# Layer 0's mixer: low weight parts by adding transfers, GpSimd's elementwise work on VectorE, table products merged

## The chip, the cores and the metric

The kernel runs on one core of one Trainium2 chip. The metric is the device time of one execution in microseconds (us). PE is TensorE, DVE is VectorE, ACT is ScalarE, POOL is GpSimd, and SP is the queue from which most loads are issued.

## What is computed

A stack of two layers on 256 context and 256 latent tokens of width 1024, all in float32. A layer normalises and modulates its input, makes one wide input projection, feeds four mixers from it, gates and sums their projections, and ends with an MLP. In layer 0 both halves of the tokens go through everything; in layer 1 the context feeds only the states of the first mixer.

```python
for l in range(2):
    h = modulate(rms_norm(x), mod[l])          # shift and scale from c @ w_mod
    z = h @ w_in[l]                            # 5 x 256 mixer inputs, 4 x 1024 gates
    y = [s5(z[0:256]), fnet(z[256:512]), pool(z[512:768]), conv(z[768:1280])]
    x = x + ga1 * (sum(sigmoid(gate[b]) * (y[b] @ w_branch[l][b]) for b in range(4)) @ w_out[l])
    x = x + ga2 * (relu(modulate(rms_norm(x)) @ w1[l]) ** 2 @ w2[l])
```

The S5 mixer is a complex linear recurrence over time with 16 groups of 64 states. The kernel does it in blocks of eight steps: it first makes tables from the parameters (powers of the decay times the input matrix B, and the output matrix C times powers), then multiplies tokens by them, scans over the blocks, and reads out.

## The kernel before, in words

**Split weights.** A weight tile is 128x1024 in float32 (512 KB). It is used as a sum of two parts in fp32r, a rounded high part `hi` and the rest `lo = w - hi`. `mm3` then issues three matmuls for each product: hi by x-high, hi by x-low, lo by x-high. A tile of 512 columns is 24 matmuls of 512 columns, one of a projection (`proj`) six.

**The stream of weights.** Class `Stream` walks one list (`plan`) of all weight tiles in the order of use. `load` (L680) starts the transfer of a tile into one of three raw buffers from SP. `high` (L689) takes a free pair of buffers and lets ACT write `hi` from the raw tile. `low` (L700), some 2.5 us later in the program's own clock, lets DVE write `lo` by a subtraction and gives the raw buffer back. There are four pairs, and a fifth is lent until shortly before the first projection. `take` (L720) hands a finished pair to PE, `release` gives it back.

**The order of work.** The program is written out by hand, engine by engine, with each queue in order. The main line is `layer` (L1285): the order string of L948 names gates (`g`), projections (`q`) and the points where a mixer's result is needed (`y`). Beside it run background tasks (generators) that `pump` (L903) advances between the matmuls of a tile. `pump` keeps an estimate of when each engine will have worked off what was issued; a task goes on only while its engines have less than `lead` microseconds of issued work left, counted from PE's present. `yield "w", t` says that the task goes on t us later.

**The tasks of layer 0's mixer.** `S5.prep` (L116) computes the small parameters on DVE. Then `tables_c` (L311) runs on POOL and `tables_b` (L265) on DVE, side by side: eight halves each, six products of 128x256 per half, followed by transposes or matmuls on PE (`products`), ACT copies and stores to scratch in DRAM (`scr_b`, `scr_c`, `scr_k`). When both are done, `S5L.run` starts: scan tables on POOL, block inputs on PE (`states`), the scan (L550) whose forward direction runs on POOL and whose backward direction runs on DVE, and the readout (L600), which loads `scr_c` again from POOL's queue. Pooling, convolution and the Fourier mixer are further tasks on DVE, PE and ACT. After the Fourier mixer's result is taken, `mods` (L1038) computes the remaining modulation columns on DVE from 80 loads of 512 KB (`w_modt`); it goes on far into the MLP.

**Layer 1's tables** are made by the same `tables_b` and `tables_c` during layer 0's MLP, all on POOL and with single buffers.

## Time and profile before

| what | value |
| --- | --- |
| time, median of 3 runs | 1207.88 us (1205.53 to 1212.44) |
| profiled execution: its own time, its span | 1209.18 us, 1207.2 us |
| PE busy | 1160.9 us (96% of the span) |
| DVE busy | 976.1 us (81%) |
| ACT busy | 517.1 us (43%) |
| POOL busy | 282.9 us (23%) |
| moved by DMA | 211.49 MB, 175 GB/s on average |
| mean granted TensorE clock | 0.986 |

The profiled execution is 1.3 us above the median and has 2.0 us outside its span. Times of rows are counted from the span's start. PE's busy time says where PE had work, not that it was at its peak; the granted clock beside it is a share of 2.4 GHz, so a mean of 0.66 over a stretch is a mixture of 1.2 and 2.4 GHz.

### The profile page before, as it was taken

The numbers are of one execution on the slowest core, as the hardware profiler recorded it, in microseconds if no ns is written. First come the engines' busy times: TensorE is split into PE (matmuls) and PEld (weight loads), VectorE is DVE, ScalarE is ACT, GpSimd is POOL, SyncE is SP. The second block draws the span as 40 slices with busy tenths as digits, with TensorE's granted clock in tenths as the row PEclk, the third lists the DMA queues.
The fourth block names the chain that finished last, engine by engine and source line by source line (L and its number), as shares of the span: only waits on it lengthen the run. The fifth ranks groups of instructions, "written<-read, shape, count | busy, mean of one in ns | idle before, by whom it ended". The sixth has DMA issues, their size and how long they took to land.

```text
span 1207.2 us, 20297 instructions
## 1 busy us (share of the span) xinstructions
PE 1160.9 (96%) x7770; PEld 1009.4 (84%) x7770; DVE 976.1 (81%) x1878; ACT 517.1 (43%) x872; POOL 282.9 (23%) x319
## 2 busy tenths in 40 slices
PE   7999897999999999999999899999899999999997
PEld 5777675777888988888887778898899999999997
DVE  6789989977999769999988883546998788867764
ACT  4534242344324365422332333346544556645543
POOL 0038656000000100166555561020520001000000
PEclk9999999999999999999999999999899999999999
DMA  9543531644674514466578774425554545555551
GB/s 366 225 144 109 180 92 52 229 156 138 212 229 156 173 37 148 140 188 230 186 245 296 249 247 180 130 98 177 173 166 167 159 160 205 177 190 179 189 182 48
DMA packets 66513, 211.49 MB, mean 175 GB/s; under 512 B 7984, under 2 KB 13616, under 8 KB 66416
## 3 DMA queue, kind: packets, MB, share of 16 engines
q1 hardware_dynamic: 55456, 183.84, 45.4%
q10 hardware_dynamic: 7696, 14.56, 3.3%
q0 software_dynamic: 3264, 11.80, 2.9%
q8 instruction: 61, 1.00, 0.3%
q14 instruction: 36, 0.29, 0.1%
HBM read 199.19 MB, written 10.98 MB: 174 GB/s over the span
## 4 chain that ended last, share of the span: by engine, by line
PE 72%; DVE 15%; POOL 3%; DMA 3%; issue 3%; ACT 3%; ACTq 0%; POOLq 0%; DVEq 0%; SPq 0%
PE bank L64 72%; DVE scan L64 5%; DVE parts L64 4%; DVE mixer L64 2%; DVE whole L64 2%; ACT parts L64 2%; POOL tables L64 1%; POOL whole L64 1%; ACT whole L64 1%; DVE windows L64 1%; POOL scan L64 1%; DMA whole<-in_w_in_dram 1%; DMA whole<-in_x_dram 0%; DMA scan<-scr_z 0%; DMA scr_c<-tables 0%
## 5 line engine op out<-in xcount | busy, mean ns | idle before, releaser
L64 PE MATMUL bank<-parts 128*128 128x512 f32 (+2 forms) x4008 | 727.2, 339 | 19.0 <-DVE parts L64 16.6
L64 PEld LDWEIGHTS bank<-parts 128*128 128x128 f32 x4008 | 616.3, 191 | 105.4 <-DVE parts L64 22.3
L64 ACT ACTIVATE parts<-whole 128x1024 fp32r<-128x1024 f32 (+1 forms) x288 | 273.7, 959 | 144.9 <-PE bank L64 73.9
L64 DVE TENSOR_TENSOR parts<-whole,parts 128x1024 fp32r<-128x1024 f32 (+1 forms) x240 | 294.0, 1233 | 16.0 <-ACT parts L64 15.6
L64 PE MATMUL bank<-hidden,parts 128*128 128x256 f32 (+1 forms) x1440 | 251.2, 335 | 0.0
L64 PEld LDWEIGHTS bank<-hidden,parts 128*128 128x128 f32 x1440 | 217.5, 188 | 29.9 <-issue 0.3
L64 DVE SCALAR_TENSOR_TENSOR whole<-whole 128x1024 f32<-128x1024 f32 (+4 forms) x188 | 175.7, 936 | 15.2 <-DMA whole<-in_w_modt_dram 12.0
L64 POOL TENSOR_TENSOR whole<-whole 128x256 f32<-128x256 f32 (+1 forms) x69 | 50.3, 743 | 347.2 <-ACT whole L64 342.2
L64 DVE SCALAR_TENSOR_TENSOR whole<-bank,whole 128x256 f32<-128x256 f32 (+1 forms) x121 | 54.7, 475 | 66.4 <-PE bank L64 66.2
L64 ACT ACTIVATE whole<-whole 128x256 f32<-128x256 f32 (+2 forms) x139 | 48.9, 388 | 107.2 <-DVE whole L64 96.4
L64 ACT ACTIVATE mixer<-bank 128x512 f32<-128x512 f32 (+1 forms) x84 | 40.7, 496 | 119.8 <-PE bank L64 110.3
L64 DVE TENSOR_TENSOR whole<-whole 128x256 f32<-128x256 f32 (+7 forms) x158 | 73.0, 467 | 16.7 <-ACT whole L64 11.7
L64 ACT ACTIVATE whole<-bank 128x512 f32<-128x512 f32 (+2 forms) x69 | 35.5, 537 | 109.1 <-PE bank L64 77.5
L64 POOL TENSOR_TENSOR tables<-tables,whole 128x256 f32<-128x256 f32 x48 | 61.4, 1287 | 37.4 <-DMA scr_c<-tables 34.9
L64 DVE TENSOR_TENSOR hidden<-whole,hidden 128x512 fp32r<-128x512 f32 (+2 forms) x77 | 53.4, 698 | 9.0 <-ACT hidden L64 2.4
L64 ACT ACTIVATE hidden<-whole 128x512 fp32r<-128x512 f32 (+2 forms) x77 | 47.1, 615 | 8.2 <-PE bank L64 2.3
L64 ACT ACTIVATE tables<-bank 128x512 f32<-128x512 f32 (+2 forms) x20 | 8.4, 422 | 92.8 <-PE bank L64 92.5
L64 POOL COPY whole<-whole 128x32 f32<-128x32 f32 x20 | 11.9, 626 | 150.3 <-DVE whole L64 150.3
L64 POOL TENSOR_TENSOR scan<-scan,whole 128x256 f32<-128x256 f32 (+3 forms) x50 | 44.0, 892 | 12.0 <-DVE scan L64 8.3
L64 DVE SCALAR_TENSOR_TENSOR scan<-scan,whole 128x512 f32<-128x512 f32 (+1 forms) x64 | 42.7, 728 | 0.0
L64 PE MATMUL bank<-merged,parts 128*128 128x256 f32 (+1 forms) x240 | 38.0, 316 | 0.8 <-DVE merged L64 0.8
L64 DVE TENSOR_TENSOR scan<-scan,whole 128x256 f32<-128x256 f32 (+5 forms) x61 | 31.5, 543 | 9.0 <-ACT whole L64 8.0
(115 smaller groups left out, 899.0 us busy)
## 6 DMA issues: line engine op xcount, KB each, us to landing
whole<-in_w_dram SPq DMA_DIRECT2D x128, 512.0 KB, 4.3
whole<-in_w_in_dram SPq DMA_DIRECT2D x84, 512.0 KB, 4.3
whole<-in_w_modt_dram SPq DMA_DIRECT2D x78, 512.0 KB, 4.1
whole<-in_w_br_dram SPq DMA_DIRECT2D x16, 512.0 KB, 4.4
whole<-in_w_out_dram SPq DMA_DIRECT2D x16, 512.0 KB, 4.2
mixer<-in_w_mod_dram SPq DMA_DIRECT2D x8, 512.0 KB, 9.7
scan<-scr_b POOLq DMA_DIRECT2D x8, 512.0 KB, 5.2
scan<-in_w_mod_dram SPq DMA_DIRECT2D x6, 512.0 KB, 9.7
```

The source lines that it names most:

```text
L64: return f(out, *a, **k)
```

## The change

In layer 0, from the ninth weight tile on up to the fourth output tile, `lo` is no longer made by DVE. ACT writes `hi`, then `-hi` into the low buffer, and a transfer from POOL's queue adds the weight tile from DRAM to what lies there. The raw buffer is free as soon as `-hi` has been issued.

`tables_b` and `tables_c` form their products for real and imaginary part at once: ACT first lays out the four operands (five or six small copies for each half), then three products of 128x512 follow in place of six of 128x256. This holds for both layers; layer 0's `tables_c` moves from POOL to DVE, and so do its scan tables and the forward direction of its scan. The sign change of C goes to ACT.

The tasks' waits change: after a table's products the task goes on when DVE is estimated to be done (`"at"`, `"u"`), the lead of DVE is 6.0 us and of ACT 3.2 us up to the S5 result of layer 0, and the readout gives its loads 12.5 us in place of 10.0.

```diff
+    def turned(self, E, out, x, y, P, space):
+        sh, t = [128, 4, 16, 8], self.K.tmp()
+        w = []
+        for i, p in enumerate(P):
+            w.append(space[:, 32 * i:32 * i + 32])
+            self.K.nc.scalar.activation(w[i].rearrange("p (r q s) -> p r q s", r=2, q=2),
+                                        bc(p[:, None], [128, 2, 2, 8]), AF.Copy)
...
+        E.tensor_tensor(ov, bc(x[:, :, :, None], sh), wv[0], op=MUL)
+        E.tensor_tensor(tv, bc(y[:, :, :, None], sh), wv[1], op=MUL)
+        E.tensor_tensor(out, out, t, op=ADD)
@@ tables_b
-            E.tensor_tensor(ba[:, 0], Bb[0], Pb[0], op=MUL)
-            E.tensor_tensor(tmp, Bb[1], Pb[1], op=MUL)
-            E.tensor_tensor(ba[:, 0], ba[:, 0], tmp, op=SUB)
-            E.tensor_tensor(ba[:, 1], Bb[0], Pb[1], op=MUL)
-            E.tensor_tensor(tmp, Bb[1], Pb[0], op=MUL)
-            E.tensor_tensor(ba[:, 1], ba[:, 1], tmp, op=ADD)
+            nc.scalar.activation(x, bb[:, :, k, qs], AF.Copy)
+            nc.scalar.activation(y[:, 0], bb[:, 1, k, qs], AF.Copy, scale=-1.0)
+            nc.scalar.activation(y[:, 1], bb[:, 0, k, qs], AF.Copy)
+            self.turned(E, BAs[i % nb], space[:, 0:64].rearrange("p (a c) -> p a c", a=4),
+                        space[:, 64:128].rearrange("p (a c) -> p a c", a=4), P, space[:, 128:192])
...
+                yield "at", done[i + 1 - nb] + 0.5
@@ tables_c
-            E.tensor_scalar(CC[:, 1], CC[:, 1], -1.0, 0.0, op0=MUL, op1=ADD)
+            nc.scalar.activation(CC[:, 1], CC[:, 1], AF.Copy, scale=-1.0)
@@ Stream
+        self.added = (8, self.index(("out", 0, 4)))
...
-                self.K.nc.scalar.activation(self.used[i][0][0], self.raw[i], AF.Copy)
+                hi, lo = self.used[i][0]
+                self.K.nc.scalar.activation(hi, self.raw[i], AF.Copy)
                 self.nhigh += 1
-                self.due.append(self.K.nc.clock["t"] + self.lag)
+                if self.adds(i):
+                    self.K.nc.scalar.activation(lo, hi, AF.Copy, scale=-1.0)
+                    self.free.append(self.raw.pop(i))
+                    self.due.append(self.K.nc.clock["t"])
+                    self.low()
+                else:
+                    self.due.append(self.K.nc.clock["t"] + self.lag)
...
-            raw = self.raw.pop(i)
-            self.K.nc.vector.tensor_sub(lo, raw, hi)
-            self.free.append(raw)
+            if self.adds(i):
+                self.K.nc.gpsimd.dma_start(lo, self.plan[i][1], accum_op=ADD)
+            else:
+                raw = self.raw.pop(i)
+                self.K.nc.vector.tensor_sub(lo, raw, hi)
+                self.free.append(raw)
@@ Model, layer, run
-        self.lead = dict(d=2.0, a=2.0, p=5.0)
+        self.lead = dict(d=6.0, a=3.2, p=5.0)
...
+                    self.lead = dict(d=2.0, a=2.0, p=5.0)
...
-            self.tab0.append(self.start(self.pre[0].tables_c(half[1], nc.gpsimd), "pa", 2.5))
+            self.tab0.append(self.start(self.pre[0].tables_c(half[1], nc.vector), "da", 2.5))
@@ readout, S5L
-                yield "w", 10.0
+                yield "w", 12.5
...
-        s.E = [K.nc.gpsimd, K.nc.vector]
+        s.E = [K.nc.gpsimd if l else K.nc.vector, K.nc.vector]
...
-            yield from s.scan_tables(nc.gpsimd)
+            yield from s.scan_tables(nc.vector)
```

How the order moves on POOL, at the place where layer 0's tables stood. In the names, `parts` holds the pairs of high and low parts, `scan` the tables and the states of layer 0's S5, `whole` the constants, raw tiles and temporaries. Before:

```order
L64 COPY whole<-whole 128x32 x9
L64 MEMSET scan 128x256 x2
L64 TENSOR_SCALAR scan<-scan 128x64
L64 TENSOR_TENSOR scan<-scan,whole 128x256
L64 TENSOR_TENSOR whole<-scan,whole 128x256
L64 TENSOR_TENSOR scan<-scan,whole 128x256 x2
```

With the change:

```order
L64 DMA parts<-in_w_in_dram 128x1024 x3
L64 COPY whole<-whole 128x32 x9
L64 DMA parts<-in_w_in_dram 128x1024
L64 DMA parts<-in_w_br_dram 128x1024
L64 DMA parts<-in_w_in_dram 128x1024 x6
L64 DMA parts<-in_w_br_dram 128x1024
L64 DMA parts<-in_w_in_dram 128x1024
L64 DMA scan<-scr_b 128x2x512 x2
L64 DMA scan<-scr_z 128x16x64
```

The products have left POOL. Its queue is now a chain of adding transfers, with the scratch loads of S5 among them, and nine copies of table powers stand ahead of all but the first three. In all 46 weight tiles get an adding transfer.

On DVE, in the middle of the same tables, where one projection's two merges fall. Before:

```order
L64 TENSOR_TENSOR scan<-scan,whole 128x256
L64 TENSOR_TENSOR mixer<-bank_65,mixer 128x512
L64 TENSOR_TENSOR parts<-whole,parts 128x1024
L64 TENSOR_TENSOR mixer<-bank_66,mixer 128x512
L64 TENSOR_TENSOR parts<-whole,parts 128x1024
L64 TENSOR_TENSOR scan<-whole 128x256
L64 TENSOR_TENSOR whole<-whole 128x256
L64 TENSOR_TENSOR scan<-scan,whole 128x256
```

With the change:

```order
L64 TENSOR_TENSOR scan<-scan,whole 128x512
L64 SCALAR_TENSOR_TENSOR scan<-scan,whole 128x512
L64 TENSOR_TENSOR mixer<-bank_65,mixer 128x512
L64 SCALAR_TENSOR_TENSOR scan<-scan,whole 128x512
L64 TENSOR_TENSOR mixer<-bank_66,mixer 128x512
L64 TENSOR_TENSOR scan<-scan 128x512
L64 TENSOR_TENSOR whole<-scan 128x512
L64 TENSOR_TENSOR scan<-scan,whole 128x512
```

The subtractions of 128x1024 (`parts<-whole,parts`) are gone from between the merges, the table products are twice as wide, and convolution steps (`SCALAR_TENSOR_TENSOR`) now stand among them.

## Rows read from the trace of the kernel before

**Rows 1.** Busy time by stage; columns are named in its first line.

```profile
core 0: us, PE busy (x) PEld busy (x) DVE busy (x) ACT busy (x) POOL busy (x), PEclk, DMA share, GB/s
75.00:212.00 137.00, 121.32 (x718) 94.57 (x717) 127.54 (x220) 49.40 (x123) 92.87 (x112) 0.95 0.32 109
212.00:400.00 188.00, 188.00 (x1090) 149.77 (x1089) 166.90 (x264) 69.00 (x96) 2.62 (x5) 0.99 0.57 190
640.00:700.00 60.00, 55.79 (x285) 43.99 (x285) 51.85 (x71) 20.71 (x36) 38.29 (x33) 0.97 0.79 264
```

**Rows 2.** Waits of PE's matmuls, stretch 70 to 215 us: total, times, longest.

```profile
PE bank L64 <- DVE parts L64: 7.8, 1, 7.8
PE bank L64 <- POOL scan L64: 3.9, 2, 2.1
PE bank L64 <- DMA scan<-scr_z: 2.2, 1, 2.2
PE bank L64 <- DVE scan L64: 1.6, 2, 1.0
```

**Rows 3.** Busy time by stretches of 5 us, columns as in rows 1.

```profile
70.00:75.00 5.00, 5.00 (x24) 4.13 (x23) 3.84 (x16) 2.06 (x3) 1.61 (x3) 1.00 0.61 196
...
130.00:135.00 5.00, 5.00 (x18) 3.87 (x16) 4.93 (x8) 3.39 (x6) 3.78 (x5) 0.66 0.27 105
...
210.00:215.00 5.00, 3.58 (x9) 2.82 (x10) 4.96 (x8) 0.15 (x1) 1.86 (x3) 0.50 0.41 135
```

**Rows 4.** Groups of DVE instructions, 75 to 212 us: busy us, mean ns.

```profile
L64 DVE TENSOR_TENSOR parts<-whole,parts 128x1024 fp32r<-128x1024 f32 x14 | 17.8, 1280 | 4.8 <-ACT parts L64 4.8
L64 DVE TENSOR_TENSOR scan<-scan,whole 128x256 f32<-128x256 f32 x22 | 15.9, 722 | 0.6
L64 DVE TENSOR_TENSOR scan<-whole 128x256 f32<-128x256 f32 x16 | 12.5, 782 | 0.0
L64 DVE TENSOR_TENSOR whole<-whole 128x256 f32<-128x256 f32 x16 | 12.3, 769 | 0.6 <-POOL scan L64 0.6
```

**Rows 5.** DVE in order of time: start us, us, instruction.

```profile
77.41 0.69 DVE L64 TENSOR_TENSOR scan<-scan,whole 128x512 f32<-128x512 f32 x1 [3.51 <-ACT whole L64]
...
115.43 0.95 DVE L64 TENSOR_TENSOR scan<-whole 128x256 f32<-128x256 f32 x1
...
121.34 0.41 DVE L64 TENSOR_TENSOR scan<-whole 128x256 f32<-128x256 f32 x1
...
175.18 1.81 DVE L64 TENSOR_TENSOR scan<-scan 128x512 f32<-128x512 f32 x1
...
210.06 0.69 DVE L64 TENSOR_TENSOR scan<-scan 128x512 f32<-128x512 f32 x1
```

**Rows 6.** Groups of ACT instructions, 75 to 212 us.

```profile
L64 ACT ACTIVATE parts<-whole 128x1024 fp32r<-128x1024 f32 x16 | 16.9, 1058 | 5.2 <-DMA whole<-in_w_in_dram 5.1
L64 ACT ACTIVATE mixer<-bank 128x512 f32<-128x512 f32 x19 | 11.4, 598 | 24.0 <-PE bank L64 23.1 <-ACT scan L64 0.8
...
L64 ACT ACTIVATE whole<-whole 128x16 f32<-128x16 f32 x25 | 2.7, 200 | 10.2 <-POOL whole L64 10.2
```

**Rows 7.** The page's DMA queues and issues: count, KB each, us to landing.

```profile
q1 hardware_dynamic: 55456, 183.84, 45.4%
...
mixer<-in_w_mod_dram SPq DMA_DIRECT2D x8, 512.0 KB, 9.7
scan<-scr_b POOLq DMA_DIRECT2D x8, 512.0 KB, 5.2
```

**Rows 8.** Groups of POOL instructions, 75 to 212 us.

```profile
L64 POOL COPY whole<-whole 128x32 f32<-128x32 f32 x7 | 5.7, 848 | 6.6 <-DVE whole L64 6.6
...
L64 POOL DMA_DIRECT2D scan<-scr_b x4 | 3.1, 766 | 17.8 <-PE bank L64 12.7 <-DMA scr_k<-scan 5.1
```

**Rows 9.** Groups of POOL instructions in layer 1's tables, 500 to 720 us.

```profile
L64 POOL TENSOR_TENSOR tables<-tables,whole 128x256 f32<-128x256 f32 x45 | 58.4, 1305 | 37.3 <-DMA scr_c<-tables 34.9
```

**Rows 10.** Waits of matmuls, stretch 630 to 700 us.

```profile
PE bank L64 <- POOL tables L64: 4.2, 3, 3.0
```

More of the change, by code (lines that the diff above doesn't have):

```diff
@@ L262, in powers @@
             yield
+    def turned(self, E, out, x, y, P, space):
[5 more added lines that the diff above has]
+                                        bc(p[:, None], [128, 2, 2, 8]), AF.Copy)
+        ov, tv = [o.rearrange("p (a c s) -> p a c s", a=4, c=16) for o in (out, t)]
+        wv = [bc(v.rearrange("p (a s) -> p a s", a=4)[:, :, None, :], sh) for v in w]
+        E.tensor_tensor(ov, bc(x[:, :, :, None], sh), wv[0], op=MUL)
+        E.tensor_tensor(tv, bc(y[:, :, :, None], sh), wv[1], op=MUL)
+        E.tensor_tensor(out, out, t, op=ADD)
     def tables_b(self, A, E):
@@ L273, in tables_b @@
         nb = 2 if l == 0 else 1
-        BAs, BATs = [A(512) for _ in range(nb)], [A(512) for _ in range(nb)]
+        BAs, BATs, spaces = [[A(w) for _ in range(nb)] for w in (512, 512, 192)]
         def products(i):
@@ L300, in tables_b @@
                 yield "w", 8.0
+            done.append(nc.clock["d"])
             if i >= nb - 1:
+                yield "at", done[i + 1 - nb] + 0.5
                 products(i + 1 - nb)
@@ L319, in tables_c @@
         nb = 2 if l == 0 else 1
-        CCs, CAs, KKs, BLs = [[A(w) for _ in range(n)] for w, n in ((128, 2), (512, nb), (240, nb), (256, nb))]
+        CCs, CAs, KKs, BLs, spaces = [[A(w) for _ in range(n)]
+                                     for w, n in ((128, nb), (512, nb), (240, nb), (256, nb), (192, nb))]
         for BL in BLs:
@@ L324, in load @@
         def load(u):
-            (nc.gpsimd if l else nc.sync).dma_start(CCs[u % 2], K.I["s5c"][l][u])
-        load(0)
-        load(1)
+            (nc.gpsimd if l else nc.sync).dma_start(CCs[u % nb], K.I["s5c"][l][u])
+        for u in range(nb):
+            load(u)
         yield "w", 2.6
@@ L354, in products @@
             nc.scalar.dma_start(K.KD[l][64 * u:64 * u + 64], KK[0:64])
-            if u < 2:
-                load(u + 2)
+            if u + nb < 4:
+                load(u + nb)
         def bufs(u, k):
-            CC = CCs[u % 2].rearrange("p (r k q c) -> p r k q c", r=2, k=2, c=16)
+            CC = CCs[u % nb].rearrange("p (r k q c) -> p r k q c", r=2, k=2, c=16)
             BL = BLs[u % nb].rearrange("p (k r q x) -> p k r q x", k=2, r=2, x=32)
@@ L376, in tables_c @@
                 P = [(base[:, r, 0, qs, 1:9] if k == 0 else rev[:, r, 1, qs, 0:8]) for r in range(2)]
[L377 to L385 removed]
+                space = spaces[(2 * u + k) % nb]
+                x, y = [space[:, j:j + 64].rearrange("p (r q c) -> p r q c", r=2, q=2) for j in (0, 64)]
+                nc.scalar.activation(x, CC[:, :, k], AF.Copy)
+                nc.scalar.activation(y[:, 0], CC[:, 1, k], AF.Copy)
+                nc.scalar.activation(y[:, 1], CC[:, 0, k], AF.Copy, scale=-1.0)
+                self.turned(E, CA, space[:, 0:64].rearrange("p (a c) -> p a c", a=4),
+                            space[:, 64:128].rearrange("p (a c) -> p a c", a=4), P, space[:, 128:192])
                 yield
@@ L388, in tables_c @@
                     yield "w", 8.0
-                todo.append((u, k))
+                todo.append((u, k, nc.clock["d"]))
                 if len(todo) == nb:
-                    products(*todo.pop(0))
+                    if nb > 1:
+                        yield "at", todo[0][2] + 0.5
+                    products(*todo.pop(0)[0:2])
                 if nb == 1:
-                    yield "w", 2.0
-        yield "w", 3.0
+                    yield "w", 2.0 + 2.0 * k
         for x in todo:
-            products(*x)
+            yield "at", x[2] + 0.5
+            products(*x[0:2])
         yield "w", 3.79
@@ L678, in lend, with adds @@
         self.lent.insert(0, (until, slots))
+    def adds(self, i):
+        return self.added[0] <= i < self.added[1]
     def load(self):
@@ L925, in said @@
                 task["cls"] = y[1]
+            elif y[0] == "u":
+                c = self.nc.clock
+                task["ready"] = max(c["t"], c[y[1]]) + y[2]
+            elif y[0] == "at":
+                task["ready"] = y[1]
             else:
@@ L1437, in layer @@
         self.flush()
-        tconv = self.start(br.conv(), "d", 4.0)
+        tconv = self.start(br.conv(), "d", 4.0 if l else 4.0)
         tasks = {2: task, 3: tconv}
@@ L1692, in run @@
         self.pre = [S5(self, 0), None]
-        half = [self.A5.sub(3600), self.A5.sub(2400)]
+        half = [self.A5.sub(3552), self.A5.sub(2656)]
         self.tab0 = []
@@ L1826, in pool @@
             yield
-        yield "w", 3.0
+        yield "u", "d", 0.5
         out = self.bufs_pool()
```

28 lines of the change are left out of this document (10 added, 18 removed).

## The prediction

> **What bounds the kernel now.** I read the table of stages first, then what PE waited for, then the groups of each engine. PE is busy in all but 46 us of the span, so only its idle time and its slow clock can be won. From 212 to 400 us, where most of layer 0's gates and projections run, PE is busy in all 188 us; nothing is to be won there. From 75 to 212 us, while S5's tables, states and scan are made, PE is busy in 121.3 of 137 us and DVE in 127.5 [rows 1]: 15.7 us of PE are lost while DVE is 93% busy. PE's waits name the same engines: 7.8 us once for a low part (`DVE parts`), 3.9 for POOL's tables, 2.2 for the load of S5's input, 1.6 for DVE's tables [rows 2]. Each stall costs twice. In 130 to 135 us, after one of the waits for POOL, the granted clock is 0.66, and in 210 to 215 us, after the longest one, 0.50, that is 1.2 GHz [rows 3]. The mean of the stage is 0.95, so about 0.05 x 137 = 6.9 us are lost to it. What can be won in this stage is 15.7 + 6.9 = 22.6 us.
>
> Why DVE is late there is seen in single instructions. A product of 128x256 takes 0.41 us at 121.34, when POOL has nothing to do, and 0.95 at 115.43, when POOL multiplies too; a sum of 128x512 in the scan takes 0.69 at 210.06 and 1.81 at 175.18 [rows 5]. So DVE and POOL take turns, and moving work to POOL buys little.
>
> In layer 1's tables (640 to 700 us) PE loses 60 - 55.8 = 4.2 us [rows 1], all of it to POOL's tables [rows 10], and 0.03 x 60 = 1.8 us of clock: 6.0 together.
>
> **The change, part by part.**
>
> *Low parts.* 46 subtractions leave DVE. 14 of them lie in the tight stage, 17.8 us of DVE [rows 4], and the wait of 7.8 us behind the scan goes with them. In its place stands a longer chain. A pair of buffers is free when PE ends a tile. ACT then evicts the gate (0.60), writes `hi` (1.06) and `-hi`, which has no row and reads a tile of the same size, so again 1.06 [rows 6]. POOL issues in about 0.77 [rows 8]: 3.5 us in all. Then the transfer lands. PE wants the pair three tiles later, and a tile of 24 matmuls takes 5.0 us (70 to 75 us, [rows 3]): 15.0 us. The landing may thus take 11.5 us. No adding transfer is in the trace. From below, a plain load of 512 KB from POOL's queue lands in 5.2 us; from above, the loads at the start, with the engines full, take 9.7 [rows 7]. I take 7, nearer to the lower end, because the stage moves little: DMA share 0.32 [rows 1]. It fits, with 4 us to spare.
>
> The engines' own time: 183.84 MB took 45.4% of 1207.2 us [rows 7], so 0.524 MB take 1.56 us of all engines. In 212 to 400 us the share is 0.57, 107 us; 29 adding transfers there (46, less the 14 of the tight stage, less the three that stand ahead of POOL's copies) add 45 us at the plain price: 152 of 188.
>
> *ACT* gains 14 x 1.06 = 15 us in the tight stage, and some 80 small copies for the tables at 0.20 each [rows 6], 16 us. With the 49.4 it has [rows 1] it is 80 us busy of 114. Hidden, as long as nothing in its queue waits.
>
> *Tables.* DVE's 48 products of 128x256 (12.5 + 12.3, and 16 at 0.72 = 11.6: 36.4 us [rows 4]) become 24 of 128x512 at 0.69 [rows 5], and the 24 from POOL are added: 48 x 0.69 = 33.1 us. The engine does twice the tables in less time.
>
> *Scan.* Both directions now run on DVE. Alone, a step costs less than half of what it costs in turns (0.69 against 1.81), so both take about what one does now; scan tables add 16 x 0.17, from steps of 128x16, 2.7 us. DVE in this stage: 127.5 - 17.8 - 36.4 + 33.1 + 2.7 = 109 us, in a stage that may shrink to 114. It stays nearly full, but convolution steps, due only later, make up much of it.
>
> *POOL's queue* is in order. Nine copies of powers, 0.85 us each [rows 8], wait for DVE, and all but three adding transfers stand behind them; later S5's loads of 0.5 to 1 MB stand between, and a load into a buffer that the scan still uses holds what is queued behind it. I charge two new stalls of 1.5 us, each with 1.7 us of clock (0.34 x 5, [rows 3]): 6.4 us.
>
> *Layer 1's tables.* Six products at 1.3 us [rows 9] become three of double width. If each still waits for one DVE instruction, they take some 6 us in place of 7.8, but five ACT copies now stand ahead of them. Between nothing and all of the 6.0 us I take half, 3.0.
>
> Sum: 1209.2 (the profiled execution) - 22.6 - 3.0 + 6.4 = 1190.0; the median lies 1.3 lower: **1189 us**. With nothing charged and all of layer 1 won: 1209.2 - 22.6 - 6.0 - 1.3 = 1179.
>
> **Rivals.**
>
> *The engines fill up.* An adding transfer reads the weight and the old low part and writes once. If it is charged for both reads it takes 2 x 1.56 = 3.1 us. Then 212 to 400 us want 107 + 29 x 3.1 = 197 us of 188, and PE, which has no slack there, waits up to 9 us: 1198. Against it: part of the 107 us is loads of modulation weights, most of which can wait. For it speaks the Trainium skill, in Collectives: The Full Stack, section "The bandwidth ceiling: the fold count and why AG ≠ RS ≠ AR": a reduction step reads two sources with two read descriptors on one ring, and measures about half the rate of a copy. No run shown so far holds such a transfer.
>
> *The low parts come too late: slower.* If the landing takes 12.5 us, each of the 46 tiles makes PE wait 1.0 us: 1179 + 46 = 1225, and the clock on top. It decides from 11.5 + 28.6 / 46 = 12.1 us, where the delays eat the 28.6 us that can be won. Against it: even the full engines at the start land in 9.7 [rows 7]. For it: POOL's queue adds its own waits to every landing.
>
> *DVE stays the limit.* It is still 109 us busy, and with a lead of 6.0 us more of its work stands ahead of the merges that free PE's banks. If half the stage's loss stays and layer 1 gives nothing: 1207.9 - 11.3 + 6.4 = 1203.
>
> That the change does not do what it says is excluded by the order: the subtractions and POOL's products are gone from where they stood.
>
> **How the numbers follow.** The forecast gets 0.64, full engines 0.10, DVE as the limit 0.14, late low parts 0.12. A change under 0.5% (6 us) can't be told from none; 1203 falls there. Faster: 0.64 + 0.10, and a little of the third, 0.75; the same 0.13; slower 0.12. The range begins at 1178, just under the full gain; it takes in 1198 and 1203 and reaches to 1212, which leaves out the late low parts and a few hundredths below.
>
> **What would show it.** Right: in the stage of S5's tables PE's idle time under 5 us and the clock over 0.98; 128x512 products on DVE at 0.69; adding transfers landing in 6 to 9 us; no wait of PE for `POOL tables` in layer 1. Wrong: PE waiting for transfers into `parts`, or a landing over 11 us (late low parts); DMA share near 1.0 from 212 us on, with PE idle there (full engines); PE waiting for DVE's `scan` or for merges (DVE the limit).

## The result and the profile after

The changed kernel takes 1239.4 us (median of 4 runs, 1236.6 to 1244.7), the kernel before 1208.8 on the same chip: a ratio of 1.026 [1.021, 1.030], slower by 31 us where 1189 us, faster, was forecast. The profiled execution spans 1234.6 us, 27.4 more than before.

The stages first. The columns are those of [rows 1], and so are the stretches. A stretch is the same time in each kernel, not the same work: a busy PE there means that the kernel gets further.

```profile
75.00:212.00 137.00, 127.08 (x756) 99.16 (x755) 107.62 (x248) 80.58 (x228) 23.13 (x33) 0.99 0.76 198
212.00:400.00 188.00, 163.84 (x935) 126.23 (x934) 136.00 (x261) 78.47 (x101) 22.86 (x28) 0.92 0.87 251
640.00:700.00 60.00, 59.75 (x288) 47.88 (x287) 49.64 (x70) 16.84 (x41) 19.33 (x13) 1.00 0.76 251
```

Against [rows 1]: S5's stage won 127.1 - 121.3 = 5.8 us of PE's idle time, and a clock of 0.99 in place of 0.95 is worth 0.04 x 137 = 5.5. The stretch where PE had been busy throughout lost 188 - 163.8 = 24.2 us, and 0.07 x 188 = 13 us of clock. Its DMA share rose from 0.57 to 0.87. Layer 1's tables won the 4 us that PE had been idle. So the loss stands in 212 to 400 us, where the forecast had seen nothing to be won and had added no wait to its sum. It is made early: PE's first matmul of 128x1 for the norm behind the output projection starts at 448.7 us in place of 415.0, 33.8 us later; behind it the changed kernel needs 785.9 us and the kernel before 792.2.

What PE's matmuls waited for in 212 to 400 us (total, times, longest):

```profile
PE bank L64 <- DVE mixer L64: 8.1, 2, 5.4
PE bank L64 <- ACT scan L64: 4.4, 2, 3.5
PE bank L64 <- DMA parts<-in_w_br_dram: 4.3, 2, 2.3
PE bank L64 <- DMA parts<-in_w_in_dram: 2.7, 2, 2.0
PE bank L64 <- DVE parts L64: 2.4, 1, 2.4
```

7.0 us are waits for adding transfers themselves (`DMA parts`), and 4.8 more in S5's stage. The largest single group, 8.1 us, is DVE's merges (`mixer`). What DVE waited for in the same stretch:

```profile
DVE whole L64 <- DMA whole<-in_w_modt_dram: 27.7, 12, 5.2
DVE whole L64 <- ACT whole L64: 13.1, 2, 12.8
DVE whole L64 <- DMA mixer<-in_w_modt_dram: 8.9, 2, 7.0
```

DVE stood still for 36.6 us, 14 times, for modulation weights from SP's queue; in the kernel before it was 0.7 us, once. Part of that is that DVE, without its subtractions, comes to the weights sooner: it takes 32 modulation columns in this stretch in place of 24. The 12.8 us are a wait for ACT, which itself waited 8.5 us for `crow`, a load that POOL's queue issues. DVE in order of time shows what stands behind such a load, at two merges that PE waited for (start us, us, instruction):

```profile
343.44 1.23 DVE L64 SCALAR_TENSOR_TENSOR whole<-whole 128x1024 bf16<-128x1024 f32 x1 [5.15 <-DMA whole<-in_w_modt_dram]
...
346.27 0.68 DVE L64 TENSOR_TENSOR mixer<-bank,mixer 128x512 f32<-128x512 f32 x1
...
391.19 1.23 DVE L64 SCALAR_TENSOR_TENSOR whole<-whole 128x1024 bf16<-128x1024 f32 x1 [1.21 <-DMA whole<-in_w_modt_dram]
...
395.48 1.22 DVE L64 SCALAR_TENSOR_TENSOR whole<-whole 128x1024 f32<-128x1024 f32 x1
...
396.83 0.68 DVE L64 TENSOR_TENSOR mixer<-bank,mixer 128x512 f32<-128x512 f32 x1
```

PE's tiles need the banks that the merges at 346.27 and 396.83 empty, and start as these end:

```profile
347.01 32.25 PE L64 MATMUL bank<-parts 128*128 128x512 f32 x134 [2.73 <-DVE mixer L64]
...
397.56 11.82 PE L64 MATMUL bank<-parts 128*128 128x512 f32 x42 [5.38 <-DVE mixer L64]
```

Ahead of the first merge DVE had stood 5.15 us for a weight. Ahead of the second it stood 1.21: there the merge waits mainly behind modulation columns that DVE is computing, two instructions of 1.2 us each, and e3 below has this wait without the price of adding.

The mean share of 0.87 hides stretches in which the engines are full. Of the 19 stretches of 10 us (the first of 8) from 212 on, nine have a share of 1.00 or more, and 17.8 of PE's 24.2 us of idle time lie in them; in the kernel before none is over 0.86. Two stretches of 20 us, columns as above:

```profile
240.00:260.00 20.00, 14.56 (x121) 9.91 (x120) 14.36 (x36) 11.82 (x15) 1.70 (x2) 0.83 1.05 301
280.00:300.00 20.00, 14.09 (x121) 10.57 (x120) 7.66 (x14) 8.63 (x12) 3.30 (x4) 0.81 1.05 283
```

The transfers by themselves: the queues of the page, and issues with count, size and median landing. They answer to [rows 7].

```profile
q1 hardware_dynamic: 55456, 183.84, 43.5%
q0 software_dynamic: 9888, 35.92, 13.2%
...
parts<-in_w_in_dram POOLq DMA_DIRECT2D x34, 512.0 KB, 8.4
...
windows<-scr_k SPq DMA_DIRECT2D x16, 64.0 KB, 11.7
```

POOL's queue q0 took 2.9% of the engines' time before, 35 us, and now 13.2%, 163 us. The 46 adding transfers thus took (163 - 35) / 46 = 2.8 us of all engines each, not 1.56. Those of `in_w_in_dram` land in 8.4 us in the median, 15.4 at the longest, and a small load from another queue, `windows<-scr_k`, now lands in 11.7 where it took 5.1; ACT waited for it, and PE for ACT's `scan`.

### The profile page after: what moved, and what is told of

Its sections match the earlier page's. It is cut to its first block, busy times and chain, and to the rows that moved or that the text cites. A ratio compares the mean times of both kernels' runs of the same rounds, so it can differ in the third digit from the quotient of the medians.

```text
span 1234.6 us, 20416 instructions
## 1 busy us (share of the span) xinstructions
PE 1170.3 (95%) x7770; PEld 1013.8 (82%) x7770; DVE 919.4 (74%) x1880; ACT 584.4 (47%) x1086; POOL 186.8 (15%) x213
## 3 DMA queue, kind: packets, MB, share of 16 engines
q0 software_dynamic: 9888, 35.92, 13.2%
## 4 chain that ended last, share of the span: by engine, by line
PE 58%; DVE 17%; DMA 12%; issue 8%; ACT 4%; POOL 1%; SPq 0%; ACTq 0%; POOLq 0%; DVEq 0%
PE bank L64 58%; DVE whole L64 6%; DMA whole<-in_w_modt_dram 5%; DVE scan L64 3%; DVE mixer L64 3%; DVE parts L64 3%; ACT parts L64 2%; DMA windows<-scr_k 1%; ACT whole L64 1%; DMA whole<-in_crow_dram 1%; DMA whole<-in_w_dram 1%; DMA scan<-scr_b 1%; DVE windows L64 1%; DMA parts<-in_w_in_dram 1%; DMA whole<-in_w_in_dram 1%
## 5 line engine op out<-in xcount | busy, mean ns | idle before, releaser
L64 DVE TENSOR_TENSOR parts<-whole,parts 128x1024 fp32r<-128x1024 f32 (+2 forms) x195 | 236.2, 1219 | 28.4 <-ACT parts L64 27.7
L64 DVE SCALAR_TENSOR_TENSOR whole<-whole 128x1024 f32<-128x1024 f32 (+4 forms) x182 | 163.0, 896 | 42.9 <-DMA whole<-in_w_modt_dram 39.5
L64 DVE TENSOR_TENSOR whole<-whole 128x512 f32<-128x512 f32 (+6 forms) x157 | 62.3, 409 | 43.5 <-ACT whole L64 38.3
L64 POOL DMA_DIRECT2D parts<-in_w_in_dram x34 | 29.6, 869 | 241.8 <-ACT parts L64 219.7
L64 POOL TENSOR_TENSOR whole<-whole 128x256 f32<-128x256 f32 (+1 forms) x38 | 22.5, 605 | 195.7 <-ACT whole L64 195.3
L64 DVE TENSOR_TENSOR scan<-scan 128x512 f32<-128x512 f32 (+4 forms) x77 | 33.1, 438 | 21.1 <-DMA scr_c<-scan 12.7
L64 ACT ACTIVATE parts<-parts 128x1024 fp32r<-128x1024 f32 x45 | 47.7, 1061 | 1.4
L64 DVE TENSOR_TENSOR scan<-scan,whole 128x512 f32<-128x512 f32 (+5 forms) x79 | 33.1, 445 | 10.8 <-ACT whole L64 6.7
L64 POOL TENSOR_TENSOR tables<-tables 128x512 f32<-128x512 f32 x16 | 22.1, 1380 | 123.2 <-ACT tables L64 75.7
```

The costliest lines, as they stand in the source:

```text
L64: return f(out, *a, **k)
```

## The experiments

Three theories were on record. **A**: the adding transfers and the modulation weights fill the DMA engines; DVE waits for the weights in its order, merges behind. **B**: the adding transfers only land late. **C**: the new order (tables and scan on DVE, longer leads) makes DVE the limit. The runs by what they keep of the change; each ratio is to the kernel before on the same chip, where its median was 1207.3 to 1208.9 us:

| run | adding tiles | scan's forward direction | tables, layer 0 | leads DVE, ACT | us | ratio to before |
|---|---|---|---|---|---|---|
| before | 0 | POOL | DVE and POOL | 2.0, 2.0 | 1208.8 | |
| changed | 46 | DVE | merged, DVE | 6.0, 3.2 | 1239.4 | 1.026 [1.021, 1.030] |
| e1 | 0 | DVE | merged, DVE | 6.0, 3.2 | 1234.2 | 1.020 [1.015, 1.024] |
| e2 | 22 | DVE | merged, DVE | 6.0, 3.2 | 1219.0 | 1.007 [1.004, 1.009] |
| e3 | 46, copied | DVE | merged, DVE | 6.0, 3.2 | 1208.3 | 0.999 [0.997, 1.002] |
| e5 | 46 | POOL | DVE and POOL | 2.0, 2.0 | 1267.7 | 1.049 [1.046, 1.052] |
| e7 | 0 | POOL | merged, DVE | 6.0, 3.2 | 1210.9 | 1.001 [1.000, 1.003] |
| e12 | 0 | POOL | merged, DVE | 2.0, 2.0 | 1224.1 | 1.014 [1.011, 1.017] |
| e9 | 8 | POOL | merged, DVE | 6.0, 3.2 | 1206.4 | 0.999 [0.998, 1.001] |
| e10 | 16 | POOL | merged, DVE | 6.0, 3.2 | 1221.0 | 1.011 [1.008, 1.014] |

### Adding or copying

e1 takes the adding transfers out; the subtractions are back on DVE.

```diff
-        self.added = (8, self.index(("out", 0, 4)))
+        self.added = (8, 8)
```

> No adding transfer at all; every low part is again a subtraction on DVE, everything else as in the change. Theory A (full engines): the adding transfers hold the 16 DMA engines, and from 212 us on, with the loads of modulation weights, they fill them; DVE waits in order for those loads and PSUM merges stand behind it. Then PE's idle time in 212 to 400 us falls from 24 to under 6 us, the DMA share there from 0.87 to 0.65 or less, and the time is 1195 to 1212 us. Theory B (late landing): the engines do not matter, each low part simply lands 8 us after its issue; it gives the same here. Theory C (the new order: longer leads, tables and scan on DVE, modulation earlier) expects 1225 us or more, since all of that is still there.

1234.2 us: neither A nor B can be the only cause (both had 1195 to 1212), and C's 1225 or more came. The stages of e1:

```profile
75.00:212.00 137.00, 135.79 (x808) 107.96 (x808) 121.19 (x216) 65.99 (x215) 10.66 (x16) 1.00 0.44 143
212.00:400.00 188.00, 168.11 (x973) 130.29 (x972) 146.81 (x285) 61.32 (x86) 2.15 (x3) 0.93 0.44 138
400.00:480.00 80.00, 59.29 (x392) 55.33 (x391) 55.12 (x122) 29.10 (x49) 6.96 (x8) 0.85 0.41 135
```

With room in the engines (0.44) PE is busy in all but 1.2 us of S5's stage and at full clock. Then DVE is late instead, as PE's waits in 212 to 480 us show:

```profile
PE bank L64 <- DVE whole L64: 16.6, 1, 16.6
PE bank L64 <- DVE scan L64: 15.2, 5, 4.8
```

The new order needs a DVE that has lost its subtractions. The 16.6 us are modulation columns that had been put off and had to be done at once.

e2 keeps the first 22 adding tiles alone.

```diff
-        self.added = (8, self.index(("out", 0, 4)))
+        self.added = (8, self.index(("in", 0, 34)))
```

> Adding transfers only for the first 22 of the 46 tiles, the ones before the loads of modulation weights begin; DVE subtracts for the other 24. A: the stage of tables and scan keeps what the change won (PE busy 127 of 137 us, clock 0.99), 212 to 400 us is as in the kernel before (PE idle under 5 us): 1185 to 1203 us, under the kernel before and under the run without any adding transfer. B: the late tiles of the first half stay, about half of the loss: 1215 to 1228. C: 1225 or more.

1219.0 us: better than none and than 46, but above A's range and in that of B. PE is busy in 178.9 of the 188 us from 212 on, where A had under 5 us of idle time. B's reason shows only in part: up to 480 us PE waits 6.0 us for adding transfers and 6.6 for DVE's scan, and in 640 to 760 us 8.9 for POOL's tables, a loss that neither theory had.

e3 leaves every transfer, buffer and order, but copies the weight in place of adding it (the low parts then hold the weights).

```diff
-                self.K.nc.gpsimd.dma_start(lo, self.plan[i][1], accum_op=ADD)
+                self.K.nc.gpsimd.dma_start(lo, self.plan[i][1])
```

> The same 46 transfers from POOL's queue, but they copy the weight over the low buffer and do not add, so the low parts are the weights themselves: the engines read and write the same tile once and do not read the old low part. A, with the second read as the price: the DMA share in 212 to 400 us falls from 0.87 to about 0.70 and the time to 1200 to 1218 us. If POOL's queue or its descriptors are the price and not the adding (B): landing stays near 8 us and the time 1230 to 1242. C: 1235.

1208.3 us, in A's range and far from those of B and C: the adding itself costs 31 us. In the profile of e3, the queue and the stages:

```profile
q0 software_dynamic: 9888, 35.92, 9.2%
```

```profile
75.00:212.00 137.00, 135.36 (x800) 106.25 (x799) 117.26 (x277) 84.13 (x231) 17.95 (x34) 1.00 0.67 212
212.00:400.00 188.00, 172.62 (x1011) 134.75 (x1010) 152.65 (x273) 90.00 (x117) 16.47 (x30) 0.98 0.83 279
```

The same packets take (110 - 35) / 46 = 1.6 us of all engines each, the price of the forecast, and land in 5.6 us. The share from 212 on is still 0.83, where A had 0.70, but only three of the 19 stretches are at 1.00 or more, so the mean share alone does not tell full engines from busy ones. And even with the transfers at the forecast price the kernel is no faster than before.

Where the 31 us are lost is seen when both are read up to the same work, PE's first matmul for the norm:

```profile
366.62 12.31 PE L64 MATMUL bank<-parts 128*128 128x512 f32 x42 [6.42 <-DVE mixer L64]
...
417.01 0.61 PE L64 MATMUL bank<-whole 128*128 128x1 f32 x4 [1.41 <-POOL whole L64]
```

That is 31.7 us before the changed kernel's 448.7. From 75 us up to there PE waits 34.1 us in the changed kernel and 17.0 in e3. PE's waits for adding transfers, and for DVE's merges, in the changed kernel:

```profile
PE bank L64 <- DVE mixer L64: 8.1, 2, 5.4
PE bank L64 <- DMA parts<-in_w_in_dram: 7.5, 4, 3.0
PE bank L64 <- DMA parts<-in_w_br_dram: 4.3, 2, 2.3
```

and in e3, where `parts<-in_w_in_dram` has 0.3:

```profile
PE bank L64 <- DVE mixer L64: 6.4, 1, 6.4
PE bank L64 <- DMA parts<-in_w_br_dram: 0.4, 1, 0.4
```

So of the 17.1 us between them 11.1 are waits for the transfers themselves, and 1.7 waits for merges. The wait of 6.42 is the one of 5.38 at the same tile; the adding does not make it. The rest of the 31 us is mostly the slow clock that comes with the waits: 0.92 in place of 0.98 from 212 to 400 us is 0.06 x 188 = 11 us. A's price is there, but the longer way to PE is the late landing that B names, not DVE's waits for the weights.

e8 measures the transfers by themselves: 8 copies from SP, 8 from POOL, 8 adding ones, each waiting for the one before, then 24 of each kind over four buffers.

```diff
+        for n in range(24):
+            nc.gpsimd.dma_start(P[n % 4], w[n % 16])
+        for n in range(24):
+            nc.gpsimd.dma_start(P[n % 4], w[n % 16], accum_op=ADD)
```

> Computes nothing of the reference: it only moves 512 KB weight tiles into SBUF, first 8 one after the other from SP, 8 from POOL, 8 adding ones from POOL, then 24 of each over four buffers. A (adding costs more of the engines): an adding transfer alone lands in 7 to 8.5 us against 5 to 5.6 of POOL's copy, and 24 in flight take 2.6 to 3.1 us apiece against 1.5 to 1.7 of a copy. B (it only lands later): 7 to 8.5 us alone, but 1.5 to 1.8 us apiece in flight. Its time stands against no other kernel's.

Its stretches: POOL's copies one by one, adding ones one by one, then copies and adding ones in flight. There is no PE in it: behind the clock of 1.00 stand the DMA share and the GB/s.

```profile
40.20:70.50 30.30, 0.00 (x0) 0.00 (x0) 4.40 (x8) 1.00 0.45 138
70.50:115.50 45.00, 0.00 (x0) 0.00 (x0) 6.88 (x8) 1.00 0.58 93
...
148.00:183.00 35.00, 0.00 (x0) 2.75 (x3) 12.51 (x25) 1.00 1.05 345
184.20:239.80 55.60, 0.00 (x0) 0.00 (x0) 19.77 (x23) 1.00 1.06 214
```

In flight, at full engines, 345 GB/s fall to 214. POOL's issues show it singly, each waiting for a buffer of the four:

```profile
190.34 0.86 POOL L64 DMA_DIRECT2D parts<-in_w_in_dram  x1 [2.64 <-DMA parts<-in_w_in_dram]
...
237.57 0.86 POOL L64 DMA_DIRECT2D parts<-in_w_in_dram  x1 [1.62 <-DMA parts<-in_w_in_dram]
```

These are 19 steps in 47.2 us, 2.49 us per adding transfer; the copies take 18 steps from 154.55 to 180.82, 1.46 us each. Alone, one behind the other, an adding transfer takes 5.6 us and a copy 3.8, both less than expected. The 2.49 us lie just under A's 2.6 to 3.1: that adding takes more of the engines, 1.7 times a copy, is shown; B's word "only", that it lands later and costs the engines nothing, falls. The Trainium skill (Collectives: The Full Stack, section "The bandwidth ceiling: the fold count and why AG ≠ RS ≠ AR") gives a reduction step about half the rate of a copy, because it reads two sources; here it was 214 of 345, 0.62. Why it is 0.62 no run shows.

e4 tests the modulation weights: the columns 16 to 39, their first 24 loads, come at half the pace.

```diff
-            yield "w", 3.02
+            yield "w", 6.0 if i < 40 else 3.02
```

> The change with the modulation columns 16 to 39 asked for every 6.0 us of program time, not every 3.0: fewer loads of 512 KB beside the adding transfers. A: DMA share in 212 to 400 us about 0.75, waits of DVE for these loads under 10 us in that stretch, PE idle there 10 us or less, time 1208 to 1224. B: unchanged, 1233 to 1242. C: about 1230, since modulation moves back to where it stood before but the rest stays.

1232.3 us, 7 less than the changed kernel, above A's range and near C's 1230. DVE's waits for the weights, 17.1 us, and the share of 0.90 miss A too. What A had right is the idle time: PE is busy in 180.5 of the 188 us from 212 on, 16.7 more, so those loads did stand in the way there, and all of the 7.5 us that it still stands idle lie in stretches of 10 us with a share of 1.00 or more. The work that was put off takes it back: 400 to 480 us has 73.4 us of PE in place of 75.7, and 640 to 760 us 114.8 in place of 119.8.

### One part of the change at a time

e5 is the kernel before with the adding transfers alone.

```diff
+        self.added = (8, self.index(("out", 0, 4)))
...
+            if self.adds(i):
+                self.K.nc.gpsimd.dma_start(lo, self.plan[i][1], accum_op=ADD)
```

> The kernel before with the adding transfers alone: tables, scan, leads and layer 1 stay as they were. A (the adding transfers fill the DMA engines and PE waits for low parts and, through DVE, for modulation weights): 1220 to 1240, PE idle by 10 us or more in 212 to 400 us, DMA share there over 0.8. C (the loss comes from POOL's work on DVE and from the new order): 1190 to 1208, no such idle time. 46 subtractions have left DVE here, so DVE's waits get shorter by either.

1267.7 us, the slowest of all, beyond A's range. S5's stage itself has fallen to 108.6 us of PE, from 121.3 [rows 1], and PE waits there for the tables that POOL makes, 13.0 us in 75 to 300. POOL's own waits in 75 to 260 us say why:

```profile
POOL parts L64 <- ACT parts L64: 46.9, 9, 8.7
POOL scan L64 <- PE bank L64: 15.7, 3, 8.9
```

Each adding transfer stands in POOL's queue until ACT has written `-hi`, and POOL's products stand behind it. So the two halves of the change need each other: the adding transfers need a POOL without other work, and, by e1, DVE can take over the tables and the whole scan only if the subtractions leave it.

e6 is the kernel before with layer 1's merged products alone.

```diff
-                        yield from self.pre[1].tables_b(self.APRE, E)
-                        yield from self.pre[1].tables_c(self.APRE, E)
+                        yield from self.pre[1].merged_b(self.APRE, E)
+                        yield from self.pre[1].merged_c(self.APRE, E)
```

> The kernel before with the merged products in layer 1's tables alone. The changed kernel had PE waiting 0.3 us for POOL's tables there in place of 4.2, and a clock of 1.00 in place of 0.97. If that is the merged products' doing, 640 to 740 us win 4 to 6 us and the kernel takes 1202 to 1205 (ratio 0.995 to 0.997). Rival: the gain comes from where the changed order leaves POOL and ACT at that time, and then the ratio is 0.999 to 1.001.

1211.5 us, 1.001 [1.000, 1.003]: no gain. In 640 to 760 us PE waits

```profile
PE bank L64 <- POOL tables L64: 5.2, 1, 5.2
```

where it lost 4.2 before [rows 10]. With the products unmerged, e5 waited 0.4 us there. So what the changed kernel won in layer 1 is not the merging by itself: with the same merged products PE is busy in all 120 us there in e1 and e12, and in 111.9 in e7. That the places of the work in time decide is likely from this, and not shown.

e7 has no adding transfer, and the scan's forward direction and the scan's tables are back on POOL.

```diff
+        self.added = (8, 8)
-        s.E = [K.nc.gpsimd if l else K.nc.vector, K.nc.vector]
+        s.E = [K.nc.gpsimd, K.nc.vector]
-            yield from s.scan_tables(nc.vector)
+            yield from s.scan_tables(nc.gpsimd)
-        yield "c", "dp" if l else "d"
+        yield "c", "dp"
```

> The changed kernel without adding transfers (1234 us) with the scan's forward direction and its tables back on POOL; merged tables stay on DVE, the leads too. C by the scan (DVE is the limit because it runs both directions): 1203 to 1215, the waits of PE for DVE's scan in 256 to 340 us (15 us) under 5. C by the leads (DVE gets background work 6 us ahead of need and merges stand behind it): 1226 to 1238, waits for DVE remain, now for other tiles.

1210.9 us, 23 less than e1: both directions on DVE were what made DVE the limit there. The stages of e7:

```profile
75.00:212.00 137.00, 134.81 (x802) 106.85 (x801) 121.05 (x192) 64.29 (x213) 40.70 (x47) 1.00 0.44 145
212.00:300.00 88.00, 79.08 (x532) 59.54 (x531) 77.36 (x164) 31.51 (x44) 17.01 (x18) 0.92 0.48 159
```

This is the clearest of all. S5's stage won 13.5 us of idle time and 6.9 of clock, nearly the whole 22.6 of the forecast, and the kernel is no faster. The next 88 us, where PE had been busy throughout before, lost 8.9 us of idle time and some 5 of clock, in waits for DVE's scan:

```profile
PE bank L64 <- DVE scan L64: 7.3, 2, 5.4
```

and layer 1's tables lost 8.1 us in place of 4.2. DVE is busy in 121 + 77 = 198 of the 225 us from 75 to 300, where the kernel before has 127.5 + 71.6 = 199: PE, as I read it, only comes sooner to a DVE that has as much to do.

e12 sets the leads of e7 back.

```diff
-        self.lead = dict(d=6.0, a=3.2, p=5.0)
+        self.lead = dict(d=2.0, a=2.0, p=5.0)
```

> The changed kernel without adding transfers, with the scan's forward direction on POOL (1211 us), and the leads of DVE and ACT at 2.0 and 2.0 us as before: what is left of the change are the merged tables on DVE. If the merged tables gave the 20 us of the table stage (PE 134.8 of 137 us, clock 1.00), the stage stays at 130 or more and the time within 6 us of 1211. If the leads gave it, PE falls back under 126 in this stage and the time is 1215 to 1230.

1224.1 us, and S5's stage at 132.3 us with a clock of 1.00: half of each expectation. The merged tables on DVE, with the tasks' changed waits that no run took out, won the stage, the leads 13 us elsewhere: without them PE waits 11.6 us for DVE's scan in all, and 14.8 at once at 429 us, for modulation columns left to the end.

### Fewer adding transfers

e9, e10 and e13 are e7 with adding transfers for 8, 16 and 6 tiles, in the gap where POOL is idle.

```diff
-        self.added = (8, 8)
+        self.added = (8, 16)
```

> The changed kernel with the scan's forward direction and its tables back on POOL, and adding transfers for 8 tiles alone (the 9th to the 16th of the plan, at 75 to 145 us), while POOL has nothing else and the DMA engines are at 0.3 to 0.45. Theory: adding transfers cost only where the engines are full or POOL's queue is blocked; here DVE is spared 8 x 1.27 = 10 us before the scan and the waits for DVE at 240 to 270 us (11 us without any adding transfer) shrink: 1198 to 1206. Rival (they cost wherever they are, by PE waiting for parts): 1211 to 1222.

1206.4 us: the same as the kernel before, and just outside the theory's range. Against e7, by the ratios, it is 2.5 us less, which the intervals do not tell from nothing. 212 to 300 us has 86.9 of 88 us of PE again, and no wait for DVE's scan is left, as DVE has eight subtractions less; but S5's stage fell to 127.8 at a clock of 0.95: PE waited 3.1 us at 81 us for a landing and 3.9 at 206 for a subtraction.

e10 goes on to the 24th tile.

```diff
-        self.added = (8, 16)
+        self.added = (8, 24)
```

> The same with 16 tiles (the 9th to the 24th, up to about 190 us). From 160 us on POOL's queue holds loads that wait for PE (23 us at 160 to 184), and the adding transfers behind them are late. Theory: worse than 8 tiles by 5 to 20 us, PE waiting for parts in 160 to 200 us. Rival (POOL's queue does no harm): better than 8 tiles by up to 8 us.

1221.0 us, as the theory had it for another reason. PE's largest wait is 9.0 us for an eviction of ACT, ACT waited 16.1 us for the scan's tables of POOL, and these came late. POOL in order of time:

```profile
162.69 0.86 POOL L64 DMA_DIRECT2D parts<-in_w_in_dram  x1 [6.76 <-ACT parts L64]
163.38 1.65 POOL L64 DMA_DIRECT2D scan<-scr_b  x2
164.87 10.68 POOL L64 COPY whole<-whole 128x32 f32<-128x32 f32 x1
175.64 4.12 POOL L64 TENSOR_TENSOR whole<-whole 128x16 f32<-128x16 f32 x15
```

The copy came late behind the adding transfer, which had waited for ACT, and then took 10.7 us.

e15 is e10 with the scan's tables on DVE.

```diff
-            yield from s.scan_tables(nc.gpsimd)
+            yield from s.scan_tables(nc.vector)
```

> 16 adding tiles with the scan's tables (16 small products and a copy) on DVE in place of POOL; the scan stays split. With them on POOL, a copy of 128x32 took 10.7 us at 165 us while DVE ran 24 convolution steps back to back, ACT waited 16.1 us for POOL and PE 9.0 us for ACT. Theory (POOL's elementwise work stands still behind DVE's two-input work, and adding transfers that shift it into such a stretch make it late): that wait goes, 1203 to 1213. Rival (the adding transfers themselves hold POOL up): PE still waits 6 us or more in 160 to 200 us, 1216 to 1222.

1212.1 us: the wait is gone, and 9 us with it. So 9 of the some 14 us that 16 tiles cost over 8 came by the scan's tables, which stand behind adding transfers in POOL's queue.

e16 measures the two engines by themselves; its streams of DVE are 20 of one of these:

```diff
+V.scalar_tensor_tensor(d[0], d[1], d[2][:, 0:1], d[0], op0=MUL, op1=ADD)
+V.tensor_tensor(d[0], d[1], d[2], op=MUL)
```

> Computes nothing of the reference: POOL does 8 copies of 128x32 and 8 products of 128x256, first alone, then while DVE runs 20 convolution-like steps of 128x512 (with a scalar), then while DVE runs 20 products of two inputs of 128x512. Theory: alone a copy takes 0.1 to 0.3 us; beside either stream of DVE POOL's first instructions take several us each or the whole stream, and DVE's own get longer while POOL's products run. Rival: they take turns one by one, so each POOL instruction takes at most about 1 us longer than alone. Its time stands against no other kernel's.

POOL's copies take 0.26 us alone (8 in 2.1), and 0.72 beside DVE (8 in 5.8); DVE's steps get longer, from 0.79 to 0.93. They take turns, as the rival said.

e17 is e16 with two accumulators.

```diff
-V.scalar_tensor_tensor(d[0], d[1], d[2][:, 0:1], d[0], op0=MUL, op1=ADD)
+V.scalar_tensor_tensor(d[3 * (i % 2)], d[1], d[2][:, 0:1], d[3 * (i % 2)], op0=MUL, op1=ADD)
```

> As the first measurement of the two engines by themselves, but DVE's 20 steps write two accumulators in turn, as the convolution does, so that no step waits for the one before it. There, with one accumulator, a step took 0.79 us alone and POOL's copies 0.72 us each beside it. Theory (POOL gets in only where DVE has a gap between two instructions): steps take about 0.67 us as in the convolution, and POOL's copies wait for several or all 20 of them: the first or the mean copy takes 2 us or more. Rival (they take turns in any case): the copies stay at 0.6 to 0.9 us and the steps at 0.8 to 1.0. Its time stands against no other kernel's.

The same holds: a step takes 0.67 us alone as in the convolution (20 in 13.3), 0.85 beside POOL, and a copy

```profile
33.30 17.08 DVE L64 SCALAR_TENSOR_TENSOR whole<-whole 128x512 f32<-128x512 f32 x20 [1.27 <-ACT whole L64]
33.84 4.91 POOL L64 COPY whole<-whole 128x32 f32<-128x32 f32 x8 [16.15 <-ACT whole L64]
```

0.61. That DVE starves POOL falls as a general rule. Why the one copy in e10 took 10.7 us stays open; its record may hold a wait that the profile does not show apart.

e13 takes the 12th to the 17th tile.

```diff
-        self.added = (8, 8)
+        self.added = (11, 17)
```

> 8 adding tiles, cut to 6: those of the 12th to the 17th tile. With 8, PE waited 3.1 us at 81 us for an adding transfer's landing, issued while the DMA engines were at 1.0 (75 to 95 us), and the granted clock fell to 0.53 behind it. Theory (an adding transfer is free where the engines have room): this wait is gone, the clock of the table stage is 0.98 or more in place of 0.95, and the kernel takes 1198 to 1204. Rival (the next one waits instead, or DVE, 3 us busier, gives it back by 270 us): 1205 to 1210.

1207.7 us, ratio 1.000 [0.998, 1.001]. The wait at 81 us is gone and the stage's clock is 0.98, but PE waits 3.4 us at 167 for an eviction, 3.3 at 253 for ACT, which had waited 2.5 for DVE's scan, and 3.3 at 278 for DVE's scan itself: the rival's range, and in the main its reason.

e18 gives e13's scan tables to DVE.

```diff
-            yield from s.scan_tables(nc.gpsimd)
+            yield from s.scan_tables(nc.vector)
```

> 6 adding tiles (1208 us) with the scan's tables on DVE in place of POOL; the scan stays split. With 6 tiles PE waited 3.4 us at 167 us for an eviction that stood in ACT's queue behind the scan's tables of POOL. Theory: this wait and its slow clock (about 1.7 us) go, 1201 to 1205. Rival (DVE, 3 us busier, makes PE wait for the scan as much later): 1206 to 1210.

1212.1 us, ratio 1.004 [1.002, 1.006]. S5's stage is at 132.1 us with a clock of 1.00, and PE then waits 6.3 us at once for DVE's scan at 273 us: the rival again, but 2 us above its range; PE also waits 6.5 us at once for layer 1's tables, which it had not foreseen.

e11 is e9 with layer 1's tables as they were before.

```diff
-                        yield from self.pre[1].tables_b(self.APRE, E)
-                        yield from self.pre[1].tables_c(self.APRE, E)
+                        yield from self.pre[1].split_b(self.APRE, E)
+                        yield from self.pre[1].split_c(self.APRE, E)
```

> The kernel with 8 adding tiles, and layer 1's tables by the six unmerged products on POOL and their two buffers for S5's C, as before. With merged products PE waited 7.0 us at once for POOL's tables in 640 to 760 us, where the kernel before lost 4.2. If the merged form with its single buffer is worse, this one wins 2 to 4 us against 8 tiles alone. Rival (the wait goes with whatever else is in the DMA queues at that time): within 1.5 us of it.

1206.1 us, 0.999 [0.997, 1.001], the lowest median of all, but no difference that can be told, as the rival had it; PE waits 6.5 us in all for layer 1's tables, and 6.9 in e9.

e14 is e13 with other pauses in layer 1: 6.5 behind B's products, and behind C's

```diff
-                    yield "w", 8.0
+                    yield "w", 10.5
```

> The same with other pauses in layer 1's tables: 6.5 us in place of 8.0 behind each product of B, 10.5 in place of 8.0 behind each of C. PE waited 6.9 us there for POOL's tables of C, whose one buffer has to be written out first. If PE only comes too early for them, the wait goes and this one is 3 to 8 us below the 6 tiles alone. Rival (the time before is set by the DMA queues and PE waits as long, only later): within 2 us of it.

1210.9 us against 1207.7 without it, outside both ranges: PE waits 4.8 us at once for POOL's tables, where e13 has 1.8. The pauses do not take the wait away, and if anything make it worse.

## Why the prediction was wrong

**The engines' own time** is the step that failed first. I took the plain price, 1.56 us of all engines, for a transfer that adds, and came to 152 of 188 us. The transfers measured 2.5 us in flight by themselves and 2.8 in the kernel; with 2.8 my own sum is 107 + 29 x 2.8 = 188 of 188. The trace has only 23 of them issued there, as PE got less far, and a share of 0.87, 164 us: full in nine stretches of ten us and not in the others. The rival "the engines fill up" came nearest to the mechanism, at 3.1 us, and I gave it 0.10. With the plain price back, e3, the 31 us are gone.

**"Most of which can wait"** is the sentence that failed with it, and it also made the rival's own price, 9 us, too small. The modulation weights can land late only if nobody waits for them. DVE does, in order, for 36.6 us (18.2 in e3), and merges that free PE's banks stand behind. By e3 this way costs PE only 1.7 us more of waits for merges; the larger harm of these loads is that they share the engines with the adding transfers, as e4 shows by 16.7 us of idle time. So the engines need not be full all the time, and the loss was 24 us of idle time and 13 of clock, not 9.

**What S5's stage loses is what the kernel can win**: this step, the 22.6 us, fails independently of the transfers. e1 and e7 won 20 us there, and e3 too, at the forecast price, and none is faster than before. DVE's work up to the scan's end did not shrink enough; PE stands idle in 212 to 400 us instead, 8.9 us in e7 and 15.4 in e3, longest for DVE's scan in the one and for a merge behind modulation columns in the other. The rival "DVE stays the limit" put its loss in the same stage and priced it at 1203; it fits e7 and in part e3, at 1208 to 1211.

**Scan.** Both directions on DVE do take about what one took in turns: from the first step to the end of the last it is 173.2 to 210.8 us before and 188.0 to 228.2 in the changed kernel, 37.6 and 40.2 us, 2.9 of these a wait for PE. That the stage's DVE time came out at 107.6 us, against 109 forecast, is luck: the stretch holds 60 convolution steps in place of 41, and the last 16 us of the scan lie behind it. The cost of both directions shows where the subtractions are there too: 23 us between e1 and e7, in 212 to 480. In the changed kernel PE waits 2.3 us for DVE's scan, and no run splits the scan there.

**New stalls.** I charged two of 1.5 us. S5's stage had five waits, 10.0 us together, the longest of 3.0 us at 82.6 us, while the loads at the start had the engines at 1.01 to 1.07. I had read a DMA share of 0.32 over the whole stage, but the first adding transfers fall in its first 20 us. DVE too stood still there, 12.7 us, for stores of `scr_c`, which landed in 5.2 us in place of 2.1. The landing, taken as 7, measured 8.4 in the median, within the 11.5 that the tiles allow, but up to 15.4. Late low parts, the rival that forecast slower, thus did not come at each of the 46 tiles; six waits, 7.0 + 4.8 us, are still most of what the adding adds to PE's waits (11.1 of 17.1 us against e3).

**Layer 1.** Twice the 3.0 us came, 4 of idle time and some 2 of clock in 640 to 700 us, but the reason was wrong: e6 has the merged products and not the gain. Its cause was not settled.

What held: DVE's and POOL's turns, as a product of 128x512 takes 0.69 us of DVE once POOL is away,

```profile
L64 DVE TENSOR_TENSOR whole<-scan 128x512 f32<-128x512 f32 x16 | 11.0, 685 | 0.0
```

merged tables on DVE win S5's stage (e7, e12); ACT's 80.6 us there against 80 forecast, though with 18 of `-hi` in it in place of 14; POOL's queue in order, which e5 and e10 show to be dearer than charged.

## What to carry to other kernels

Price an adding transfer by what it takes of the engines, not by its size. Ask at the stretch where the engines are busiest how late the transfers land when they are full for 10 us, not on the mean, and who waits for the other loads, in which order, and what stands behind. A stage that loses time is worth its loss only if the engine that makes it late gets less to do up to the next point where the others need it; otherwise the wait turns up one stage later. An instruction that an in-order queue holds for another engine charges its wait to all that is behind it.

## What the runs showed of the hardware

An adding transfer of 512 KB into SBUF took 2.49 us of all engines in flight where a copy from the same queue took 1.46 (214 against 345 GB/s), and 5.6 us where a copy took 3.8 when each waited for the one before. A DVE step of 128x512 that adds to the accumulator of the step before took 0.79 us, and 0.67 when two accumulators alternate. Beside such a stream a POOL copy of 128x32 took 0.6 to 0.7 us in place of 0.26, and DVE's steps 0.15 to 0.19 more on average.
